# Two unused 32-byte pieces that shift the on-chip placement of a two-block transformer kernel

## The chip, the cores and the metric

The kernel runs on one core of one Trainium2 chip. The metric is the device time of one execution in microseconds (us); the kernel before takes 3251.84 us, the median of three runs (3248.97 to 3255.56). All data are fp32 in DRAM; a working copy lies in the core's on-chip memory, 128 partitions wide, and every tile has one start address that is the same in all partitions.

## The reference

Two transformer blocks follow one another on 256 tokens of width 2048. Cut to what matters:

```python
# block 1
xn = rmsnorm(h, attn_norm)
proj = xn @ w_in                                  # 2048 x 11776
q_a, k_a, v_a, q_r, k_r, v_r, g_r, gate_a, gate_r = split(proj)
y_a = sliding_window_attention(...) @ w_attn_branch
y_r = retention(...) @ w_ret_branch
h = h + (sigmoid(gate_a) * y_a + sigmoid(gate_r) * y_r) @ w_out
hn = rmsnorm(h, ffn_norm)
# PEER: 8 heads x 16 experts per token out of 16384, chosen by top-k of hn @ w_query
u, vv = expert_down[idx], expert_up[idx]          # rows of 2048
h = h + einsum(gates * gelu(einsum(hn, u)), vv)
h = rmsnorm(h, final_norm)
# block 2
z = rms_norm(h, mix_norm) @ w_in_2                # q, k, v, forget gates, recurrent branch
h = h + concat(forgetting_attention(q, k, v, f), rg_lru(conv(rx)) * gelu(rg)) @ w_out_2
h = h + hierarchical_moe(rms_norm(h, ffn_norm_2)) # 32 experts, top 1 group, top 2 in it
h = h + sigmoid(rms_norm(h, ple_norm) @ w_ple_gate) * (p @ w_ple_up)
```

## The kernel before

**One product, three matmuls.** TensorE reads its operands as float32r, a rounded fp32. To keep fp32 accuracy each operand is split into a rounded part `hi` and a rest `lo` (`split`, `split_w`): ScalarE casts the raw weights to `hi` (L251), VectorE subtracts to get `lo` (L252). Each product is then three matmuls into one accumulator: hi by hi, hi by lo, lo by hi. A matmul has a stationary operand, loaded first by LDWEIGHTS (128 by 128 here), and a moving operand that is streamed through (512 columns in most of them).

**Which operand lies where.** Five pools are opened first, in this order: `cst` (constants and small vectors that stay), `big` (seven buffers of 16 KB: activations and their split parts, gathered rows), `sm` (small scratch), `wr` (three raw weight tiles of 8 KB), `ws` (two pairs of `hi` and `lo` of the weights, 4 KB each). Behind them each phase opens pools of its own (`wk...` for work tiles, `wr...` and `ws...` for more weight buffers). A pool begins where the one before it ends, so the size of `cst` and `sm` sets the addresses of all the others.

- `mm_nat` (L272, matmuls L280, L281, L282): the activations in `big` are stationary, the weights in `ws` move, 512 columns. It serves the big input projection (`pj`), the branch products (`pb`), the output products (`pwo`), q and k of block 2 (`pqk`) and the closing gate (`pgt`). For v of block 2 (`pv`) the move is 344 columns wide: a pair of k tiles lies in one `ws` tile, the second 1376 bytes behind the first.
- `mm_tr` (L284, L291 to L293): weights stationary, 256 columns of activations in `big` moving.
- The dense pass over PEER's up table (L805 to L807): coefficients in work tiles (`wk`) are stationary, weights in `ws` or work tiles move, 512 columns. Beside it GpSimd gathers further rows and VectorE adds them.
- The experts of block 2: `gate_up` (L1262, L1279 to L1281) has sorted tokens `xs` in `big` as stationary operand; `down` (L1295, L1304 to L1306) has hidden rows `hhl` in a work tile. Weights in `ws` move, 512 columns, in both.
- PEER's down part gathers one row of 8 KB per token and expert into `big` (L609) and VectorE takes its dot product with `hn` (L619).

**What sets the order.** Each engine works through its own instructions in program order. Weight loads are issued by SyncE, gathers by GpSimd; a load waits until the buffer that it fills has been read.

Of the kernel before, what the change touches and what calls it, by code (L numbers as in the profile page):

```python
# [65 lines left out]
NPU = (7, 5)  # steps of the per-layer embedding's input part before and inside the routing of the experts  # L66
UA = 3  # gathered units added per expert group
NC0 = 1  # chunks of token tile 0's coefficients that stay on chip
# [7 lines left out]
def build(ctx: ExitStack, tc: tile.TileContext, A, out, taps=None, stop=None):  # L76
# [13 lines left out]
    def new_phase(name, raws=0, splits=0, e8=2):  # L90
        """working memory of one phase; raws / splits more buffers for the weight stream"""
        phase.close()
        env["wk"] = phase.enter_context(tc.tile_pool(name="wk" + name, bufs=2, reuse_waits="tile"))
        env["raw"] = [wr0] * 3
        env["split"] = [ws0] * 2
        if raws:
            env["raw"] += [phase.enter_context(tc.tile_pool(name="wr" + name, bufs=raws, reuse_waits="tile"))] * raws
        if splits:
            env["split"] += [phase.enter_context(tc.tile_pool(name="ws" + name, bufs=splits, reuse_waits="tile"))] * splits
        env["ri"] = env["si"] = 0  # L100
        env["e8"] = e8
# [25 lines left out]
    cc = cst.tile([P, NKEEP], F32, name="cc")  # L127
    nc.sync.dma_start(cc[:, 0:128], A["c_const"][:, 0:128])
    vecs = w4([P, P], name="vecs")
    nc.scalar.dma_start(vecs[0:16, :], A["attn_norm"].rearrange("(r c) -> r c", c=P))  # L130
    # input and first weights
# [48 lines left out]
    # gains of the final norm times those of the first norm of block 2  # L180
# [13 lines left out]
    def rsqrt_to(dst, v, n, tag):  # L194
        """dst = v ** -0.5 ([P, n])"""
        if n <= 4:
            G.tensor_tensor(out=dst, in0=v, in1=mhalf[:, 0:n], op=ALU.pow)  # L197
            its = 1
        else:
            d = dst.bitcast(I32)  # L200
            V.tensor_scalar(d, v.bitcast(I32), 1, None, op0=ALU.logical_shift_right)
            V.tensor_scalar(d, d, -1.0, float(0x5F3759DF), op0=ALU.mult, op1=ALU.add)
            its = 3
        tmp = sm.tile([P, n], F32, tag="rs" + tag, name="rs")
        for _ in range(its):
            V.tensor_tensor(out=tmp, in0=dst, in1=dst, op=ALU.mult)
            V.scalar_tensor_tensor(out=tmp, in0=tmp, scalar=-0.5, in1=v, op0=ALU.mult, op1=ALU.mult)
            V.scalar_tensor_tensor(out=dst, in0=tmp, scalar=1.5, in1=dst, op0=ALU.add, op1=ALU.mult)
# [9 lines left out]
    def rstd_from(ss, tag):  # L218
        """ss [P, 2, 4] sums of squares -> rstd [P, 2]"""
        r = cst.tile([P, 2], F32, name="r" + tag)  # L220
        v = sm.tile([P, 2], F32, tag="rstdv", name="rstdv")
        V.tensor_reduce(out=v, in_=ss, axis=AX.X, op=ALU.add)
        V.tensor_scalar(v, v, 1.0 / D, EPS, op0=ALU.mult, op1=ALU.add)  # L223
        rsqrt_to(r, v, 2, "n")
        return r
# [7 lines left out]
    def split(hi, lo, src, scale=None):  # L233
        """hi + lo = src (* scale); hi is rounded to float32r, lo holds the rest"""
        if scale is None:
            return (S.copy(hi, src),
                    V.tensor_tensor(out=lo, in0=src, in1=hi.bitcast(F32), op=ALU.subtract))
        return (S.mul(hi, src, scale),  # L238
                V.scalar_tensor_tensor(out=lo, in0=src, scalar=scale, in1=hi.bitcast(F32),  # L239
                                       op0=ALU.mult, op1=ALU.subtract))  # L240
# [14 lines left out]
    def load_w(src, n=4, w=512):  # L255
        """src [n*128, w] in DRAM -> raw tile [P, n, w]"""
        raw = raw_tile([P, n, w], "raw")
        nc.sync.dma_start(raw, src.rearrange("(k p) n -> p k n", p=P))
        return raw

    def wsplits(W, c0, c1, k0, nk, rot=0, loaded=()):
        """yields (k index, hi [P, w], lo [P, w]) over the k tiles of W[:, c0:c1], the first rot of them last"""
        loaded = list(loaded)
        for g in [*range(rot, nk, 4), *range(0, rot, 4)]:
            n = min(4, nk - g)
            raw = loaded.pop(0) if loaded else load_w(W[(k0 + g) * P:(k0 + g + n) * P, c0:c1], n, c1 - c0)
            for j in range(0, n, 2):
                hi, lo = split_w(raw[:, j:j + 2, :], [P, 2, c1 - c0])
                for i in range(2):
                    yield k0 + g + j + i, hi[:, i, :], lo[:, i, :]  # L270

    def mm_nat(ps, xhi, xlo, W, c0, c1, k0=0, nk=NK, xk=lambda k: k, first=True, last=True, loaded=()):  # L272
        """ps [P, 2, w] (+)= x @ W[:, c0:c1] with tokens on partitions"""
# [10 lines left out]
    def mm_tr(ps, xhi, xlo, W, c0, rot=0):  # L284
        """ps [P, 4, 256] = (x @ W[:, c0:c0+512]) with columns on partitions"""
# [15 lines left out]
    def transposed_split(hi, lo, src, gains, kts=range(NK), n=1):  # L301
        """hi/lo [P, NK, 256] <- transposes of src [P, 2, D] times per-feature gains"""
        for k0 in kts[::n]:
            if k0 % 2 == 0:
                ps = pst("ptr")
            for k in range(k0, k0 + n):
                for t in range(2):
                    o = (k % 2) * 256 + t * P
                    TE.transpose(ps[:, o:o + P], src(t, k), ident)  # L309
            for k in range(k0, k0 + n):  # L310
                o = (k % 2) * 256
                r = split(hi[:, k, :], lo[:, k, :], ps[:, o:o + 256], gains(k))
        return r

    # ================= block 1: projections =================
# [14 lines left out]
    def rope(ps, nh):  # L330
        """ps [P, 2, nh*128] raw projection -> roped, normalised [P, 2, nh, 128] in SBUF"""
# [11 lines left out]
    def heads_T(dst, o, nh, scale=1.0):  # L343
        """dst [P(d), nh, 256] <- o [P(tok), 2, nh, 128]"""
# [18 lines left out]
    for b in range(2):  # L363
        ps = proj(b * 512)
        if b == 0:
            # small constants, once the first products are under way
# [170 lines left out]
    # ================= PEER =================  # L537
# [88 lines left out]
    def key_rows(t):  # L626
        """keys of token tile t with (head, choice) on partitions: [P, 2, token]"""
# [14 lines left out]
    def onehots(dst, kT, tk, n):  # L642
        """dst [P, n, 128] = second keys of n tokens"""
        # 1 where key - iota is 0, else max(1 - (key - iota) ** 2, 0) = 0
# [4 lines left out]
    def coef_chunk(kT, cT, c, oh=None, pool=lambda tk: False):  # L649
        """coefficients of 32 tokens as [second key, first key, token]"""  # L650
# [65 lines left out]
    def onehots_ahead(kT, oh1):  # L716
        """one-hot second keys of most of token tile 1, in buffers that are idle until the dense part"""
# [27 lines left out]
    # rows of 512 columns, the last of the 4 of an expert  # L745
# [26 lines left out]
    def coef_split(ig):  # L772
        """coefficients of the 4 x 128 experts of group ig, experts on partitions: hi, lo [P, 4, 256]"""
# [52 lines left out]
    # final norm of block 1 and first norm of block 2; their scales go to the results  # L826
# [21 lines left out]
    def log1p_of(dst, u, n, tag):  # L848
        """dst = log(1 + u) for 0 <= u <= 1 ([P, n])"""
# [12 lines left out]
    # softplus(-lam) * 8 per channel  # L862
# [23 lines left out]
    for b in range(2):  # L886
        pq = acc("prx").rearrange("p a b -> p (a b)").rearrange("p (m t) -> p m t", m=4)
        mm_tr(pq, zhi, zlo, W2, 3080 + b * 512, 12)
        if b == 0:
# [11 lines left out]
            # r4 of every token on all partitions  # L901
# [57 lines left out]
    v2_ = wv[:, 1, :].rearrange("p (t c) -> p t c", t=2)  # L959
    qkTs = bigt([P, 2, 2, 4, T], name="qkTs")  # L960
    for b in range(3):
        # the columns of v, then the 8 of the forget gates
# [19 lines left out]
    def bias_row(hd):  # L982
        """[tril mask - c_s (keys 0:128) | -c_s (keys 0:128) | tril mask - c_s (keys 128:256)]"""
# [93 lines left out]
    for b in range(4):  # L1077
# [21 lines left out]
        # rows of h for the sort into slots, features in the order of the expert weights  # L1099
# [9 lines left out]
    # the part of the per-layer embedding that depends on its input alone  # L1109
# [27 lines left out]
    # ================= mixture of experts: routing =================  # L1137
# [7 lines left out]
    # 4 groups, 4 of filling, 32 experts  # L1145
# [45 lines left out]
    # in range: group * 128 + rank; beyond: 512 + (rank - 128)  # L1191
# [35 lines left out]
    # group sizes (on every partition); at most one group has more than 128 tokens  # L1227
# [17 lines left out]
    # ================= mixture of experts: experts =================  # L1245
# [4 lines left out]
    def sort(pr, k0, k1):  # L1250
        """rows of h in the slots of two groups, transposed, times the norm gain"""
# [10 lines left out]
    def gate_up(ge_, e, x_, rs_, cm_, between=lambda c: None):  # L1262
        """hidden rows of expert ge_ for 128 slots, times their weights, transposed (hi, lo)"""
# [56 lines left out]
    def run_experts(items, between=lambda i, c: None):  # L1320
        """items: (expert index, position 0..7, x, rstd, weights, PmT) in order, 8 to a group of slots"""
# [28 lines left out]
    def between(i, c):  # L1350
        """the sort, spread over the first experts"""
# [17 lines left out]
    # the first weights of the per-layer embedding  # L1369
# [7 lines left out]
    # tokens beyond the 128 slots of their group  # L1377
# [32 lines left out]
    # ================= per-layer embedding =================  # L1410
# [58 lines left out]
```

## Time and profile before

| what | value |
|---|---|
| median of three runs | 3251.84 us (3248.97 to 3255.56) |
| span of the profiled execution | 3250.5 us |
| TensorE matmul busy | 2585.5 us (80%), 12368 instructions |
| VectorE busy | 2536.2 us (78%) |
| ScalarE busy | 1540.2 us (47%) |
| GpSimd busy | 874.5 us (27%) |
| DMA mean | 276 GB/s, 898.20 MB |

The span is that of one execution under the profiler and lies 1.3 us under the median. The matmuls are pipelined: one of 512 columns is shown with a duration of about 0.39 us while the next starts 0.23 us later, so the time that one costs is read from the distance between starts in the timeline, and not from its duration. The granted clock of TensorE (PEclk) is the share of full speed that it was given in a stretch; 1.00 is the higher of its two levels, 2.4 GHz.

### The profile page before, as it was taken

What the parts mean: (1) busy time and instruction counts of PE and PEld (TensorE: products, weight loads), DVE (VectorE), ACT (ScalarE), POOL (GpSimd) and SP (SyncE); (2) the same over time, 40 slices, a digit from 0 to 9 for tenths busy, and PEclk for the clock granted to TensorE, in tenths of its full rate; (3) what the DMA queues carried; (4) which work ended last, traced back from release to release, by engine and by line L of the source; (5) the groups of instructions that cost most, each with busy time, mean ns of one, the idle gap of its engine ahead of it and who ended that gap; (6) DMA issues with size and microseconds to landing.
All of it is one profiled execution on the core that took longest, in us unless ns stands there. A gap on an engine that the chain in (4) does not pass through costs nothing. (4 is left out here: it accounts for less than half of the span.)

```text
span 3250.5 us, 35193 instructions
## 1 busy us (share of the span) xinstructions
PE 2585.5 (80%) x12368; PEld 2137.8 (66%) x12368; DVE 2536.2 (78%) x3682; ACT 1540.2 (47%) x2212; POOL 874.5 (27%) x575
## 2 busy tenths in 40 slices
PE   8999999999920004400399999999999999999999
PEld 7788788888820003300378888889887787878777
DVE  6656544445899999999988888887575789999974
ACT  5533444444310104442244444457445677777763
POOL 0000000000276686667766666620000000000000
PEclk9999999999965555555699999999999999999999
DMA  6454555555899899989799999964654599999964
GB/s 235 150 178 159 181 181 187 189 207 190 309 376 358 329 421 369 400 336 414 290 310 335 332 335 333 335 240 148 203 181 137 213 336 339 374 341 374 340 230 157
DMA packets 302521, 898.20 MB, mean 276 GB/s; under 512 B 20736, under 2 KB 42240, under 8 KB 268288
## 3 DMA queue, kind: packets, MB, share of 16 engines
q1 hardware_dynamic: 226560, 542.88, 47.3%
q0 software_dynamic: 57760, 335.65, 27.0%
q10 hardware_dynamic: 18016, 17.35, 1.6%
q8 instruction: 98, 1.61, 0.2%
q14 instruction: 87, 0.71, 0.1%
HBM read 887.42 MB, written 8.39 MB: 276 GB/s over the span
## 5 line engine op out<-in xcount | busy, mean ns | idle before, releaser
L252 DVE TENSOR_TENSOR wlo<-raw,whi 128x1024 fp32r<-128x1024 f32 (+1 forms) x538 | 648.3, 1208 | 467.9 <-ACT whi L251 464.1
L251 ACT CAST whi<-raw 128x1024 fp32r<-128x1024 f32 (+1 forms) x538 | 557.0, 1036 | 706.0 <-PE pj L282 267.8
L619 DVE CUSTOM_DVE_ANT_0 row<-row,hn 128x2048 f32<-128x2048 f32 x256 | 578.4, 2282 | 8.9 <-DMA row<-in_peer_expert_down_dram,eidx 7.7
L610 POOL DMA_INDIRECT row<-in_peer_expert_down_dram,eidx x256 | 503.5, 1967 | 270.4 <-DVE dots L619 96.9
L197 POOL TENSOR_TENSOR r<-rstdv,mhalf 128x2 f32<-128x2 f32 x5 | 4.5, 891 | 1535.7 <-DVE rstdv L223 1535.7
L610 POOL DMA_INDIRECT urow<-in_peer_expert_up_dram,eidx x256 | 322.4, 1259 | 196.9 <-DVE h L769 143.3
L252 DVE TENSOR_TENSOR wlo<-rawg,whi 128x1024 fp32r<-128x1024 f32 x256 | 313.2, 1225 | 41.9 <-ACT whi L251 37.4
L251 ACT CAST whi<-rawg 128x1024 fp32r<-128x1024 f32 x256 | 269.3, 1053 | 104.7 <-PE pgu L1281 75.8
L280 PE MATMUL pj<-whi,xhi 128*128 128x512 f32 x736 | 293.0, 398 | 1.3 <-ACT whi L251 1.3
L281 PE MATMUL pj<-wlo,xhi 128*128 128x512 f32 x736 | 292.3, 397 | 0.0
L282 PE MATMUL pj<-whi,xlo 128*128 128x512 f32 x736 | 291.8, 397 | 0.0
L637 PE MATMUL pcf<-cc,pk 128*128 128x128 f32 x2 | 0.9, 462 | 344.1 <-DVE pk L624 344.1
L637 PEld LDWEIGHTS pcf<-cc,pk 128*128 128x128 f32 x2 | 0.4, 183 | 344.9 <-issue 179.2
L1280 PE MATMUL pgu<-wlo,xs 128*128 128x512 f32 x512 | 203.2, 397 | 3.1 <-DVE wlo L252 3.1
L1279 PE MATMUL pgu<-whi,xs 128*128 128x512 f32 x512 | 203.4, 397 | 0.0
L1281 PE MATMUL pgu<-whi,xs 128*128 128x512 f32 x512 | 202.9, 396 | 0.0
L769 DVE SCALAR_TENSOR_TENSOR h<-urow,pk,h 128x512 f32<-128x512 f32 x256 | 191.6, 749 | 4.4
L252 DVE TENSOR_TENSOR wlo<-rawd,whi 128x1024 fp32r<-128x1024 f32 x128 | 154.1, 1224 | 15.7 <-ACT whi L251 11.2
L280 PEld LDWEIGHTS pj<-whi,xhi 128*128 128x128 f32 x736 | 138.2, 188 | 34.2 <-ACT whi L251 1.7
L282 PEld LDWEIGHTS pj<-whi,xlo 128*128 128x128 f32 x736 | 138.1, 188 | 32.7
L281 PEld LDWEIGHTS pj<-wlo,xhi 128*128 128x128 f32 x736 | 138.1, 188 | 32.4
L251 ACT CAST whl<-raw 128x1024 fp32r<-128x1024 f32 x96 | 101.1, 1054 | 114.2 <-PE ua L807 82.4
(547 smaller groups left out, 6287.2 us busy)
## 6 DMA issues: line engine op xcount, KB each, us to landing
raw<-in_w_in_dram SPq DMA_DIRECT2D x124, 1024.0 KB
raw<-in_peer_expert_up_dram SPq DMA_DIRECT2D x96, 1024.0 KB
rawg<-in_w_expert_gate_dram SPq DMA_DIRECT2D x128, 512.0 KB
rawg<-in_w_expert_up_dram SPq DMA_DIRECT2D x128, 512.0 KB
rawd<-in_w_expert_down_dram SPq DMA_DIRECT2D x64, 1024.0 KB
raw<-in_w_out_dram SPq DMA_DIRECT2D x32, 1024.0 KB
raw<-in_w_ret_branch_dram SPq DMA_DIRECT2D x16, 1024.0 KB
raw<-in_w_peer_query_dram SPq DMA_DIRECT2D x16, 1024.0 KB
```

What stands on the lines that cost most here:

```text
L197: G.tensor_tensor(out=dst, in0=v, in1=mhalf[:, 0:n], op=ALU.pow)
L251: S.copy(hi, raw)
L252: env["last"] = V.tensor_tensor(out=lo, in0=raw, in1=hi.bitcast(F32), op=ALU.subtract)
L280: TE.matmul(ps[:, t, :], h_, hi, start=st, stop=False)
L281: TE.matmul(ps[:, t, :], h_, lo, start=False, stop=False)
L282: env["mm"] = TE.matmul(ps[:, t, :], l_, hi, start=False, stop=en)
L610: G.indirect_dma_start(out=dst, out_offset=None, in_=src, in_offset=bass.IndirectOffsetOnAxis(ap=idx, axis=0))
L619: V.tensor_tensor_reduce(out=row[:, i, :], in0=row[:, i, :], in1=hn[:, t, :], scale=1.0, scalar=0.0, op0=ALU.mult, op1=ALU.add, accum_out= ...
L769: V.scalar_tensor_tensor(out=h[:, t, 1536:2048], in0=row[:, k, :], scalar=coef[:, t, c0 + k:c0 + k + 1], in1=h[:, t, 1536:2048], op0=ALU.m ...
L1279: TE.matmul(o_, xh, hi[:, :, i, :], start=k == 0, stop=False)
L1280: TE.matmul(o_, xh, lo[:, :, i, :], start=False, stop=False)
L1281: TE.matmul(o_, xl, hi[:, :, i, :], start=False, stop=k == NK - 1)
```

## The change

Two tiles of 8 fp32 numbers are added that nothing reads or writes, one in `cst` behind `cc` and one in `sm`. A tile in `sm` is there twice (`bufs=2`), so `cst` grows by 32 bytes and `sm` by 64. Every other line of the diff drops a comment or a docstring; behind L126 all lines move down by two.

```diff
     cc = cst.tile([P, NKEEP], F32, name="cc")
+    cst.tile([P, 8], F32, name="pad")
+    sm.tile([P, 8], F32, tag="pad", name="pad")
     nc.sync.dma_start(cc[:, 0:128], A["c_const"][:, 0:128])
```

The instructions of all five engines, their order, their shapes and their waits are the same as before. What differs is the start of the tiles. In the built programs, in bytes per partition:

| tiles | before | after | before mod 256 | after mod 256 |
|---|---|---|---|---|
| `cc` (in `cst`, ahead of the piece) | 16512 | 16512 | 128 | 128 |
| `big`, seven buffers in steps of 16384 | 23008 | 23040 | 224 | 0 |
| `wr`, three in steps of 8192 | 140960 | 141056 | 160 | 0 |
| `ws`, `hi` and `lo`, in steps of 4096 | 165536 | 165632 | 160 | 0 |
| work tiles of the phases, first one | 181920 | 182016 | 160 | 0 |
| `hhl` (experts, down) | 192160 | 192256 | 160 | 0 |
| `chi` (PEER up) | 207520 | 207616 | 160 | 0 |
| second k tile of a 344-wide weight pair (first `ws` tile) | 166912 | 167008 | 0 | 96 |

By 512 bytes the remainders after are 0 for `big` and 256 for `wr`, `ws` and the work tiles; before, 480 and 160.

## Rows read from the trace of the kernel before

**Rows 1.** The page: span, and the granted TensorE clock in 40 slices.

```profile
span 3250.5 us, 35193 instructions
...
PEclk9999999999965555555699999999999999999999
```

**Rows 2.** Busy time by stretch: PE, PEld, DVE, ACT, POOL; then PEclk, DMA share, GB/s.

```profile
81.00:812.60 731.60, 731.58 (x3269) 588.48 (x3269) 391.17 (x477) 316.38 (x388) 6.22 (x9) 1.00 0.53 180
...
975.00:1560.00 585.00, 69.30 (x261) 55.94 (x261) 573.69 (x957) 146.64 (x380) 402.61 (x208) 0.51 0.96 377
1645.00:2150.00 505.00, 505.00 (x2229) 418.31 (x2228) 437.95 (x613) 239.10 (x368) 309.69 (x246) 1.00 0.97 336
2195.00:2520.00 325.00, 317.64 (x1813) 276.44 (x1812) 214.00 (x371) 178.71 (x257) 0.00 (x0) 1.00 0.50 168
2600.00:3090.00 490.00, 485.02 (x2127) 389.75 (x2126) 444.70 (x427) 371.93 (x404) 0.00 (x0) 1.00 0.95 351
```

**Rows 3.** Timeline of PE, block 1, 430 to 450: first and last of 87.

```profile
429.76 0.39 PE L281 MATMUL pj<-wlo,xhi 128*128 128x512 f32 x1
...
449.83 0.39 PE L280 MATMUL pb<-whi,rhi 128*128 128x512 f32 x1
```

**Rows 4.** Timeline of PE, PEER's up part, 1800 to 1820: first and last of 90.

```profile
1799.82 0.39 PE L805 MATMUL ua<-whi,chi 128*128 128x512 f32 x1
...
1819.99 0.39 PE L807 MATMUL ua<-whi,clo 128*128 128x512 f32 x1
```

**Rows 5.** Timeline of PE, experts, 2700 to 2714: six steps of down, 47 of gate_up.

```profile
2700.49 0.39 PE L1306 MATMUL oa<-whi,hhl 128*128 128x512 f32 x1
...
2701.85 0.39 PE L1306 MATMUL oa<-whi,hhl 128*128 128x512 f32 x1
2702.07 0.40 PE L1279 MATMUL pgu<-whi,xs 128*128 128x512 f32 x1
...
2713.04 0.39 PE L1281 MATMUL pgu<-whi,xs 128*128 128x512 f32 x1
```

**Rows 6.** Timeline of PE, 344 columns: starts of three k tiles, six matmuls each.

```profile
2268.17 0.32 PE L280 MATMUL pv<-whi,zhi 128*128 128x344 f32 x1
...
2269.11 0.32 PE L280 MATMUL pv<-whi,zhi 128*128 128x344 f32 x1
...
2270.07 0.32 PE L280 MATMUL pv<-whi,zhi 128*128 128x344 f32 x1
```

**Rows 7.** Groups of PE by line and shape: busy, mean ns, idle before them.

```profile
L280 PE MATMUL pj<-whi,xhi 128*128 128x512 f32 x736 | 293.0, 398 | 1.3 <-ACT whi L251 1.3
...
L1279 PE MATMUL pgu<-whi,xs 128*128 128x512 f32 x512 | 203.4, 397 | 0.0
...
L1304 PE MATMUL oa<-whi,hhl 128*128 128x512 f32 x256 | 101.5, 396 | 0.0
...
L805 PE MATMUL ua<-whi,chi 128*128 128x512 f32 x256 | 100.1, 391 | 0.5 <-ACT chi L236 0.5
...
L291 PE MATMUL pq<-hhi,whi 128*128 128x256 f32 x256 | 72.5, 283 | 0.0
```

**Rows 8.** Groups of DVE by line and shape: one operation at shifts of 4 bytes.

```profile
L917 DVE SCALAR_TENSOR_TENSOR rnx<-rnx,vt 128x255 f32<-128x255 f32 x8 | 3.5, 477 | 0.0
L917 DVE SCALAR_TENSOR_TENSOR rnx<-rnx,vt 128x253 f32<-128x253 f32 x8 | 3.5, 476 | 0.0
```

**Rows 9.** DMA queue of weights, 406 to 487 and 2330 to 2400: packets, MB, share.

```profile
q1 hardware_dynamic: 7458, 14.78, 53.5%
...
q1 hardware_dynamic: 5458, 10.82, 45.8%
```

**Rows 10.** DMA queue of gathers, 1143 to 1215 and 1480 to 1540: packets, MB, share.

```profile
q0 software_dynamic: 4155, 30.26, 101.3%
...
q0 software_dynamic: 3393, 24.67, 100.7%
```

**Rows 11.** DMA queue of weights in the experts, 2762 to 2844: packets, MB, share.

```profile
q1 hardware_dynamic: 8230, 30.49, 99.0%
```

## The prediction

> **What bounds the kernel now.** I read the page's slices first, then busy time by stretch, and then went down to the distance between the starts of matmuls, because nothing but addresses changes and no view of waits can show that.
>
> The stretches [rows 2] fall into three kinds. In block 1 (81 to 812.6) the matmuls are busy for 731.58 of 731.60 us at the full granted clock, with DMA at 0.53 and VectorE at 391 us: TensorE is the only bound. The first half of block 2 (2195 to 2520) is alike, 317.64 of 325 us, DMA 0.50. In PEER's up part (1645 to 2150) and in the experts (2600 to 3090) TensorE is full as well (505 of 505, 485 of 490), but DMA stands at 0.97 and 0.95, so a faster TensorE meets a second limit at once. PEER's gathers (975 to 1560) are VectorE's: 573.69 of 585 us, TensorE 69 us at a granted clock of 0.51.
>
> A full TensorE need not be TensorE at its peak, so I took what one matmul costs from start to start. In block 1, 86 steps take 449.83 - 429.76 = 20.07 us, 233.4 ns each [rows 3]. In PEER's up part 89 steps take 1819.99 - 1799.82 = 20.17 us, 226.6 ns each [rows 4]. These are the same instruction (128 by 128 stationary, 512 columns, float32r) at the same full clock: 560 cycles of 2.4 GHz against 544. The experts show both figures within 14 us [rows 5]: down takes (2701.85 - 2700.49)/6 = 226.7 ns, gate_up right behind it (2713.04 - 2702.07)/47 = 233.4 ns. Weights come through the same buffers in both, DMA is busy in both. What differs is where the stationary operand lies. In the groups at 233.4 ns (L280 to L282, L1279 to L1281) it is in `big`, 224 past a multiple of 256, while the moving one is at 160. In those at 226.7 (L805 to L807, L1304 to L1306) both are at 160.
>
> The 344-column matmuls give a second handle [rows 6]. Their stationary operand is in `big` throughout, the moving one lies at 160 for one k tile and at 0 for the next. Six matmuls take 2269.11 - 2268.17 = 0.94 us for one and 2270.07 - 2269.11 = 0.96 us for the other, 156.7 and 160.0 ns. (The rounding of one start is 0.01 us; the pattern 0.94, 0.96 repeats over the following tiles.) In cycles that is 376 against 384, or 32 over the 344 columns against 40; with 512 columns it is 32 over against 48. So addresses matter, the better state is 32 cycles over the columns, and it was reached in two ways: with both operands at one remainder, or, as I read the order of the pairs, with the moving operand on a multiple of 256. After the change both hold in all of the groups at 233.4.
>
> **The change part by part.** Instructions added: none; removed: none; waits: the same. Each term is a number of matmuls by 233.4 - 226.7 = 6.7 ns.
>
> - Block 1. `pj` has 736 matmuls on each of the three lines [rows 7]; `pb` has 192 and block 1's `pwo` 128 in groups of the same form. (736 + 192 + 128) x 3 = 3168, by 6.7 ns: 21.2 us. All of it lies on the path: PE idles 1.3 us for ScalarE before the 736 of L280 [rows 7], and the two splitting engines have room, 316 and 391 us of 731 [rows 2]. What is late next is nothing: DMA would go from 0.53 to 0.55.
> - Block 2 outside the experts. Block 2's `pwo`, `pqk` and `pgt` with 128 each, x 3 = 1152: 7.7 us. Same reasoning, DMA 0.50 in the first part.
> - Experts, gate_up. 512 x 3 = 1536 [rows 7]: 10.3 us if TensorE alone decides. DMA's mean of 0.95 over 490 us [rows 2] would rise to 0.97 and fits on the mean, but in 82 us in the middle the weights' queue already takes 99.0% of the 16 engines [rows 11]; there a faster TensorE waits for weights. Bounds 0 and 10.3; I take half, 5 us, since the mean leaves room for all and the middle for almost nothing.
> - Experts, down: 256 x 3 = 768, at 226.7 in [rows 5]. 0 taken; should they start at 233.4 behind every gate_up, at most half of 768 x 6.7, 2.6 us.
> - PEER's up part: 2304 matmuls (256 on each of three lines for `ua` from one kind of buffer [rows 7], as many from the other, and half as many each for `ub`). At 226.6 now: 0.
> - `mm_tr`: 512 x 3 = 1536 of 256 columns (`pq` [rows 7] and two groups of 128). The moving operand goes from 224 to 0. No pair of rows tells whether these can be faster; by the same excess per column the end is 1536 x 3.35 = 5.1 us, the other end 0. I take 0, since [rows 7] show nothing unequal there.
> - 344 columns: 288 matmuls. The first k tile of a pair moves to 0 and the second to 96, so the better and the worse half change places: 0, give or take 0.5 us.
> - VectorE and ScalarE: operands move by 32 or 96 bytes. One operation ran at shifts of 4 to 12 bytes in 477 and 476 ns [rows 8], so I price all of them at 0. This is the term that the gathers' stretch rests on (573.69 us of VectorE): 1% there would be 5.7 us either way.
> - DMA: destinations move from 224 or 160 to 0. On the reading side two layouts can be compared. Rows of block 1's table have a pitch that is a multiple of 256 in DRAM, those of block 2's a pitch of 80 x 256 + 32. A packet took 81 us x 16 x 0.535 / 7458 = 93.0 ns in the one and 70 x 16 x 0.458 / 5458 = 94.0 in the other [rows 9], about 1%. I price the writing side at 0.
>
> [...]
>
> Sum: 21.2 + 7.7 + 5 = 33.9 us off the profiled span of 3250.5 [rows 1], 3216.6. The median is 1.3 above that span, so 3218 us.
>
> **The rivals.**
>
> *No change (about 3251).* The two spacings are due to something else that goes with the groups: the source buffers, the accumulator, the way the stationary operand is strided. For it: I infer from a few placements, none of which is the new one (0 for both, and by 512 still 0 against 256). Against it: [rows 6], where only the moving address alternates. To this case belongs a gain on DMA alone. [...] VectorE bounds most of the gathers, and DMA only where its queue takes all of the time: 72 and 60 us at 101.3 and 100.7% [rows 10]. [...]
>
> [...]
>
> *Slower (3272).* The spacing of 226.7 belongs to the offset 160 itself, or to some pairing that the new grid breaks: operands that all start on a multiple of 256 collide, and these groups fall to 233.4 and the others stay. Place: L805 and L1304. Price: 2304 x 6.7 = 15.4 and 768 x 6.7 = 5.1, together 20.5 us, and all on the path, since TensorE is full there [rows 2]: 3251.8 + 20.5 = 3272. It decides when L805 has 233 ns between starts. For it: those stationary and moving operands leave exactly the layout that gives 226.7 now. Against it: they keep equal remainders, and the moving operand at 0 was the better one in [rows 6].
>
> *Much faster (3170).* The 32 cycles that remain are an address cost too. At 512 cycles, 213.3 ns, all groups gain; half of it, 220 ns, gives block 1 and 2 (4320 matmuls) 13.4 x 4320 = 58 us, and the up part and the experts what DMA leaves, 3% of 505 and 5% of 490, up to 40. A sum near 80, 3170. For it: every starting address is off the grid today but one. Against it: that one ([rows 6], moving at 0) still had 32 over.
>
> **How the numbers follow.** The forecast 0.50, no change 0.24, slower 0.16, much faster 0.07, and 0.03 for gains and losses that cancel to a few us. One such measurement can tell about 0.2%, 6.5 us, from no change. Faster: 0.50 + 0.07 and a third of the rest, 0.58. Same: 0.26. Slower: 0.16. The likeliest case alone runs from 3205 (with all of gate_up, down and `mm_tr`: 33.9 + 5.3 + 2.6 + 5.1 = 46.9) to 3235 (half of the sum). The range goes from 3200 to 3273, so that it holds no change and the slower case as well and leaves out the much faster one and some tails.
>
> **What would show it.** In the profile after: starts in block 1's 512-column matmuls 226.7 ns apart, block 1's stretch 21 us shorter, the experts' between 0 and 10; L805 still at 226.6; the 344-column pairs with 0.94 and 0.96 in exchanged places; mean durations of L252, L619 and L251 unchanged; the mean packet of the weights' queue unchanged. I am wrong if block 1 keeps 233.4 (then addresses weren't it), if L805 rises (slower), if any spacing falls under 226, or if VectorE's L619 moves.

## The result, and the profile after

The changed kernel takes 3213.97 us (median of 4 runs, 3209.80 to 3219.45) where the kernel before, on the same chip, takes 3251.30: a ratio of 0.9884, 95% interval 0.9870 to 0.9898. On a second occasion it was 3214.33 and 0.9888 (0.9873 to 0.9903). The forecast was 3218 us, so 33 to 34 us of gain, and some 37 came.

The page, with the same two rows as [rows 1]: the span is 32.8 us shorter, the clock the same.

```profile
span 3217.7 us, 35193 instructions
...
PEclk9999999999965555555699999999999999999999
```

The timeline of PE in block 1, first and last of 90 (line numbers are two higher than before):

```profile
429.63 0.39 PE L283 MATMUL pj<-wlo,xhi 128*128 128x512 f32 x1
...
449.81 0.39 PE L282 MATMUL pb<-whi,rhi 128*128 128x512 f32 x1
```

(449.81 - 429.63)/89 = 226.7 ns, where [rows 3] gave 233.4. In PEER's up part nothing has moved, 20.17/89 = 226.6 as in [rows 4]:

```profile
1799.73 0.39 PE L808 MATMUL ua<-whl,chi 128*128 128x512 f32 x1
...
1819.90 0.39 PE L807 MATMUL ua<-whl,chi 128*128 128x512 f32 x1
```

In the experts gate_up, the second half of [rows 5], goes from 233.4 to (2688.54 - 2679.70)/39 = 226.7 ns:

```profile
2679.70 0.39 PE L1283 MATMUL pgu<-whi,xs 128*128 128x512 f32 x1
...
2688.54 0.39 PE L1283 MATMUL pgu<-whi,xs 128*128 128x512 f32 x1
```

The 344-column pairs of [rows 6] hardly alternate any more. By the starts in the trace the two k tiles of a pair took 0.960 and 0.940 us before and mostly take 0.950 and 0.943 after. The first two:

```profile
2248.02 0.32 PE L282 MATMUL pv<-whi,zhi 128*128 128x344 f32 x1
...
2248.96 0.32 PE L282 MATMUL pv<-whi,zhi 128*128 128x344 f32 x1
...
2249.90 0.32 PE L282 MATMUL pv<-whi,zhi 128*128 128x344 f32 x1
```

In the groups of [rows 7] the durations shrink by 5 to 6 ns where a group gained, while that of `pq` in `mm_tr` grows by 5:

```profile
L282 PE MATMUL pj<-whi,xhi 128*128 128x512 f32 x736 | 289.4, 393 | 1.3 <-ACT whi L253 1.3
...
L1281 PE MATMUL pgu<-whi,xs 128*128 128x512 f32 x512 | 200.0, 391 | 0.0
...
L293 PE MATMUL pq<-hhi,whi 128*128 128x256 f32 x256 | 73.7, 288 | 2.0 <-ACT whi L253 2.0
```

For a balance I took the mean distance between successive starts in each group, leaving out steps over 300 ns (200 in `mm_tr`), which are waits:

| group | matmuls | before, ns | after, ns | difference x matmuls, us | forecast, us |
|---|---|---|---|---|---|
| block 1: `pj`, `pb`, `pwo` | 3168 | 233.3 | 226.7 to 227.2 | -20.0 | -21.2 |
| block 2: `pqk`, `pwo`, `pgt` | 1152 | 233.3 | 226.8 to 227.8 | -6.8 | -7.7 |
| gate_up | 1536 | 233.3 | 227.2 | -9.4 | -5 |
| down | 768 | 229.6 | 227.7 | -1.5 | 0 |
| PEER up | 2304 | 226.7 | 226.7 | 0 | 0 |
| `mm_tr` | 1536 | 117.8 | 120.0 | +3.4 | 0 |

That is 34.3 us. One stage adds to it: from the last `pq` matmul to the first of the up part, in which VectorE and the gathers decide, 717.0 us went by before and 713.0 after (714.2 on the second occasion).

The two together come to 38.3, which is more than the 32.8 by which these two profiles differ: the table prices every matmul as if all of it were on the path. Cut into stages, the same two profiles give, in us: block 1 up to the first `pq` -18.6, `pq` +4.7, the gathers' stage -4.0, the up part +1.6, `prx` with `prg` -2.0, the rest of block 2 up to the experts -1.9, the experts -11.0, the closing gate to the end -2.5, and +1.1 in the pieces between. The profiled execution after was the slowest of its four (3219.45); the repeat, which ran 7 us shorter, gives -17.7, +1.3, -2.8, -0.2, -1.4, -3.3, -9.3, -5.0 and -1.3.

### The profile page after: what moved, and what is told of

The parts are those of the page before. It is cut to its first block, busy times and chain, and to the rows that moved or that the text cites. A ratio compares the mean times of both kernels' runs of the same rounds, so it can differ in the third digit from the quotient of the medians.

```text
span 3217.7 us, 35193 instructions
## 1 busy us (share of the span) xinstructions
PE 2555.4 (79%) x12368; PEld 2141.8 (67%) x12368; DVE 2535.2 (79%) x3682; ACT 1542.9 (48%) x2212; POOL 879.8 (27%) x575
## 5 line engine op out<-in xcount | busy, mean ns | idle before, releaser
L621 DVE CUSTOM_DVE_ANT_0 row<-row,hn 128x2048 f32<-128x2048 f32 x256 | 579.7, 2291 | 6.1 <-DMA row<-in_peer_expert_down_dram,eidx 5.7
L254 DVE TENSOR_TENSOR wlo<-rawg,whi 128x1024 fp32r<-128x1024 f32 x256 | 313.1, 1225 | 35.1 <-ACT whi L253 10.3
L1281 PE MATMUL pgu<-whi,xs 128*128 128x512 f32 x512 | 200.0, 391 | 0.0
L1283 PE MATMUL pgu<-whi,xs 128*128 128x512 f32 x512 | 199.2, 389 | 0.0
```

Of the source, the lines that this page charges most:

```text
L254: env["last"] = V.tensor_tensor(out=lo, in0=raw, in1=hi.bitcast(F32), op=ALU.subtract)
L621: V.tensor_tensor_reduce(out=row[:, i, :], in0=row[:, i, :], in1=hn[:, t, :], scale=1.0, scalar=0.0, op0=ALU.mult, op1=ALU.add, accum_out= ...
L1281: TE.matmul(o_, xh, hi[:, :, i, :], start=k == 0, stop=False)
L1283: TE.matmul(o_, xl, hi[:, :, i, :], start=False, stop=k == NK - 1)
```

## The experiments

Three theories stood at the start. 1: the distance between the starts of the stationary and the moving operand decides, counted by 256 bytes. 2: the moving operand has to start on a multiple of 256. 3: the stationary operand at 224 is the fault by itself. Each of the first three kernels keeps the condition of one theory and breaks the others.

**Only the piece in `cst`.** `big` comes to 0, `ws` and the work tiles to 192: the distance stays.

```diff
+    cst.tile([P, 8], F32, name="pad")
```

> Only the piece in cst: big starts at a multiple of 256, ws and the work tiles at 192 past one. Theory 1 (the distance between stationary and moving operand decides, by 256 bytes): the distance in the groups with the stationary operand in big stays 64 as before, so 512-column matmuls of L280 stay at 233 ns and the time at 3251 us. Theory 2 (the moving operand has to start on a multiple of 256): 192 is none, 233 ns, 3251 us; should a multiple of 64 be enough, 226.7 ns and 3214. Theory 3 (the stationary operand in big at 224 was the fault by itself): 226.7 ns, 3214 us. PEER's up part keeps equal remainders: 226.6 ns by theory 1.

3248.98 us against 3254.33, ratio 0.9987 (0.9977 to 0.9997). Block 1's 87 starts are (449.88 - 429.82)/86 = 233.3 ns apart:

```profile
429.82 0.39 PE L283 MATMUL pj<-whi,xlo 128*128 128x512 f32 x1
...
449.88 0.39 PE L282 MATMUL pb<-wlo,rhi 128*128 128x512 f32 x1
```

Theory 3 falls: the stationary operand is at 0 and nothing is gained in the matmuls. The few microseconds that were gained, 4 by the ratio with an interval from 1 to 7, come up again below.

**Only the piece in `sm`.** `big` stays at 224, the rest comes to 224: distance 0, far off the grid of 256.

```diff
+    sm.tile([P, 8], F32, tag="pad", name="pad")
```

> Only the piece in sm: big stays at 224 past a multiple of 256, ws and the work tiles come to 224 as well, off every grid of 64. Theory 1 (distance): distance 0, so L280 at 226.7 ns and about 3214 us, the whole gain. Theory 2 (moving operand on a multiple of 256): no gain, 233 ns, 3251 us; the up part may even get worse. Theory 3 (stationary operand at 224 at fault): no gain, 3251 us, and the up part, whose stationary operand comes to 224, goes to 233 ns, 15 us more, 3266.

3221.27 us, ratio 0.9903 (0.9886 to 0.9920); 90 starts, (449.99 - 429.81)/89 = 226.7 ns:

```profile
429.81 0.39 PE L281 MATMUL pj<-whi,xhi 128*128 128x512 f32 x1
...
449.99 0.39 PE L283 MATMUL pb<-whi,rlo 128*128 128x512 f32 x1
```

Theory 2 and theory 3 fall, theory 1 stands. Whether the whole gain is here can't be told from the time: the kernel before took 3254.33 beside it, so that the change's ratio of 0.9884 would have given about 3217, and the two intervals overlap.

**Moving operand on the grid.** `big` at 224, the rest where the change puts it.

```diff
+    sm.tile([P, 24], F32, tag="pad", name="pad", bufs=1)
```

> An unused piece of 96 bytes in sm alone: big stays at 224, ws and the work tiles come to a multiple of 256, as they are after the change. Theory 1 (distance, here 224): no forecast of its own for a distance of 224; in the 344-column pairs of before this distance gave 156.7 against 160.0 ns, so L280 would be near 226.7 and the time near 3214 to 3220. Theory 2 (moving operand on a multiple of 256): 226.7 ns, 3214 us. Theory 3 (stationary at 224 at fault): 233 ns, 3251 us.

3249.98 us, ratio 0.9991 (0.9981 to 1.0000); 87 starts, (449.85 - 429.78)/86 = 233.4 ns:

```profile
429.78 0.39 PE L282 MATMUL pj<-wlo,xhi 128*128 128x512 f32 x1
...
449.85 0.39 PE L281 MATMUL pb<-whi,rhi 128*128 128x512 f32 x1
```

Theory 2 falls here too. Theory 1 had no figure for a distance of 224, and my guess for it from 344 columns, near 226.7, missed. This also disposes of my reading of [rows 6], by which a moving operand at 0 was the better one as such.

**A map of start addresses.** Matmuls alone, all else left out.

> Leaves out the whole computation: matmuls alone, 30 back to back for each pair of start addresses of stationary and moving operand in steps of 32 bytes, over 512 bytes with 512 columns, over 256 bytes with 344 and 256 columns. Theory 1 (distance): the distance between starts of 512-column matmuls is 226.7 ns on the diagonal of equal remainders and larger off it, repeating each 256 bytes or less along both axes, and depends on the difference alone. Theory 2 (moving on the grid): 226.7 in the columns of moving starts at 0 and 256 whatever the stationary start. Theory 3: 226.7 or 233 by the stationary start alone. A fourth outcome is that all pairs give one figure; then the two figures need something of the kernel that this one lacks.

Mean distance between the last 15 starts of each cell, in ns, read from the trace; the 512-byte map repeats by 256 along both axes to 1 ns but for four cells, so rows of its first corner stand for it (stationary start down, moving start across, 512 columns):

```
          0     32     64     96    128    160    192    224
  0   226.6  233.4  228.9  233.4  232.4  234.3  233.4  233.4
 32   233.4  226.6  233.5  228.9  233.4  232.4  234.3  233.4
 64   233.4  233.4  226.6  233.4  228.9  233.4  233.4  234.3
160   233.4  232.4  234.3  233.3  233.4  226.7  233.2  228.9
224   233.5  228.7  233.5  232.4  234.3  233.3  233.4  226.6
```

Equal remainders give 226.7 in every cell, a moving operand 64 further on 228.9, all else 232 to 234. Of the four cells that don't repeat, two lie at a distance of 64 (stationary at 0 or 256, moving at 320) and give 233.3. The kernel before was the cell 224, 160: 233.3. With 256 columns the diagonal is among the worst instead: 120.0 ns, and 113.3 to 120.1 off it; the cell of `mm_tr` before (160, 224) gives 117.8, the kernel's own figure. With 344 columns the cells lie between 153 and 160, the diagonal at 157.6 to 157.8 but for one cell (64, 64) at 153.4.

**The up part set apart.** A change in the opposite sense, in a stage that the edit left alone.

```diff
     new_phase("p")
+    env["wk"].tile([P, 8], F32, tag="pad", name="pad", bufs=1)
```

> The changed kernel with one more unused piece of 32 bytes, in the work pool of PEER's phase only: the coefficients chi and clo and the split weights whl of the up part come to 32 past a multiple of 256, the ws tiles stay on one. Nothing else moves. Theory 1 (distance by 256 bytes, as in the map): the matmuls of the up part that move whi and wlo of ws (1152 of 2304, distance 224) go from 226.7 to 233.4 ns, those that move whl (distance 0) stay; 1152 x 6.7 = 7.7 us, about 3222 against 3214. Rival (the up part is bound by transfers or by VectorE's additions as soon as the matmuls change, and the spacing there is no price): the spacings as above, but no more than 2 us on the time. Rival (the grid of 256 decides): all 2304 off 226.7, 15 us.

3221.09 us beside 3214.33 of the changed kernel beside it, 6.8 more. The matmuls on `whi` and `wlo` step by (1805.05 - 1799.68)/23 = 233.5 ns. Those on `whl` begin with steps of 230 and settle at (1810.52 - 1807.80)/12 = 226.7:

```profile
1799.68 0.40 PE L808 MATMUL ua<-whi,chi 128*128 128x512 f32 x1
...
1805.05 0.40 PE L810 MATMUL ua<-whi,clo 128*128 128x512 f32 x1
1805.29 0.39 PE L808 MATMUL ub<-whl,chi 128*128 128x512 f32 x1
...
1807.80 0.39 PE L810 MATMUL ub<-whl,clo 128*128 128x512 f32 x1
...
1810.52 0.39 PE L810 MATMUL ub<-whl,clo 128*128 128x512 f32 x1
```

The intervals of the two whole times overlap, so the stage has to decide. From its first to its last `ua` matmul it took 528.4 us here, and 519.1 to 521.4 in the seven other kernels and repeats. So distance is a price on the path there too, and neither transfers nor VectorE hide it.

**A distance of 64.**

```diff
+    cst.tile([P, 8], F32, name="pad")
+    sm.tile([P, 32], F32, tag="pad", name="pad", bufs=1)
```

> big on a multiple of 256, ws and the work tiles 64 past one: for the 512-column matmuls of L280 and gate_up the moving operand lies 64 behind the stationary one, for mm_tr (weights stationary) 64 ahead of it. If the map carries over to the kernel: 512 columns at 228.8 ns (most cells of that distance) or 233.4 (the cell of exactly these remainders by 512), 256 columns at 113.3 ns instead of 120.0. Against the changed kernel: 5856 x 2.2 = 12.9 us or 5856 x 6.7 = 39 us lost, 1536 x 6.7 = 10 us gained, so 3217 or 3243 us. If the map does not carry over: 3214 (mm_tr and L280 as after) or 3251.

3224.75 us, ratio 0.9922 (0.9908 to 0.9935). The spacings came as in most cells of that distance, 89 starts at (449.96 - 429.82)/88 = 228.9 ns in block 1 and, with 256 columns, 73 at (2247.89 - 2239.73)/72 = 113.3. The cell of exactly these remainders by 512 (0 and 320) has 233.3 in the map, so a single cell doesn't carry over to the kernel. And the time is 10 us over the changed kernel and not 3:

```profile
429.82 0.39 PE L284 MATMUL pj<-whi,xlo 128*128 128x512 f32 x1
...
449.96 0.39 PE L282 MATMUL pb<-whi,rhi 128*128 128x512 f32 x1
...
2239.73 0.28 PE L293 MATMUL prg<-zhi,whi 128*128 128x256 f32 x1
...
2247.89 0.28 PE L293 MATMUL prg<-zhi,whi 128*128 128x256 f32 x1
```

Set beside the repeat of the changed kernel, block 1 up to the first `pq` lost 5.8 us (777.7 against 771.9), near what its spacing says, but `pq` itself gained only 1.9 (110.7 against 112.6) and `prx` with `prg` 0.7 (106.1 against 106.8), of 8.4 that their spacing is worth. In `mm_tr` part of what a shorter matmul saves turns into waiting. PE's wait in `pq` for VectorE's `wlo` is 8.8 us in the repeat and 11.9 here:

```profile
PE pq L295 <- DVE wlo L254: 8.8, 15, 2.3
...
PE pq L295 <- DVE wlo L254: 11.9, 14, 2.6
```

**The changed kernel again.**

> The changed kernel unaltered, beside the others on the same chip: 3214 us, 0.988 to 0.989 of before. If its gain were chance of one chip, the ratio would go towards 1.

3214.33 us, ratio 0.9888: the gain is the same to 0.1%.

**Fine steps.** Matmuls alone.

> Leaves out the whole computation: matmuls alone. First, 512 columns with the distance in steps of 4 bytes from -68 to 68: theory 1 in its sharp form has 226.7 ns at distance 0 alone and 233 already at 4 bytes; in its coarse form a plateau as wide as some piece of memory (up to 32 bytes either way, since the first map went in steps of 32). Should some distance fall under 226.7, there is more to gain. Second, stationary starts alternate between 0 and 96 and moving starts with them or against them. If a matmul's own stationary operand has to be at distance 0, alternating together gives 226.7 and against each other 233; if the stationary operand that is loaded meanwhile for the next matmul has to be at distance 0, it is the other way round. Third, widths 128 to 512 at distances 0, 96 and 192: if distance 0 costs 32 cycles over the columns at every width, it is the worst of the three at 256 and the best at 512.

No distance of 35 is under 226.6, so the much faster case that I had as a rival is not there. There is no plateau either, and 0 is not the only distance at 226.7: -4, 28 and 60 have it too. With 512 columns and the stationary operand at 128, moving operand minus stationary above, mean of the last 15 steps in ns below:

```
 -16    -12     -8     -4      0      4      8     12     16     20     24     28     32
233.3  240.0  233.4  226.7  226.7  236.6  233.3  228.9  231.9  236.0  233.3  226.7  233.3
```

The program goes through all distances twice. Two distances came out differently in the two passes, -68 with 226.7 and 230.2 and -60 with 233.3 and 240.0, so the two addresses alone don't fix the step.

Alternating both starts between 0 and 96 together gave 234 ns, alternating them against each other 230. By a matmul's own distance the first would be 226.7; so that is not what is paid for. By the distance to the weights loaded meanwhile the second would be 226.7, and it is only half way there. With 128 and with 192 columns the step is 111.5 to 111.9 ns at all three distances tried, so something other than the columns sets it there. Above that the best distance changes with the width. Of the three (0, 96 and 192), 0 is the best at 384 columns (173.3 against 176.7 and 176.8), no better or worse at 320 (146.7 each) and the worst at 448 (206.7 against 205.3 and 202.3).

**One odd matmul in 16.** To see whose distance it is.

> Leaves out the whole computation: 512-column matmuls alone, both operands at remainder 0, but one in 16 has its stationary or its moving operand 96, 32 or 116 bytes further on. Theory A (a matmul pays for the distance between its own two operands): with the stationary operand odd in number 8, the distance from start 8 to start 9 rises from 226.7 to 234 ns, and the same one with the moving operand odd. Theory B (it pays for the distance to the weights that are loaded for the next matmul while it streams): with the stationary operand odd in number 8, the distance from start 7 to start 8 rises, by some 7 ns at 96, and with the moving operand odd that from 8 to 9. Theory C (a state of the stream that needs several equal matmuls): no single distance rises, several do, before or behind.

Distances from start to start in ns; number 8 is the odd one, the same in each repeat but for 1 ns:

```
step from             6    7    8    9   10   11   12   13   14   15
stationary +96      227  229  230  236  229  232  231  227  226  227
stationary +32      227  235  228  233  231  226  227  227  226  227
stationary +116     227  231  231  230  236  229  232  231  227  226
moving +96          227  226  236  230  236  228  233  231  226  227
moving +32          227  226  236  233  233  236  224  231  236  228
```

An odd stationary operand is felt one matmul early, in number 7, which streams while the weights of number 8 are loaded (in the kernel before, the load for the matmul that starts at 440.26 us begins at 440.03 and takes 0.19, beside the matmul that starts at 440.03); an odd moving operand is felt in its own. That is the place that theory B names, though not its size: at 96 the step from 7 rises by 2 ns and not by 7. And one odd matmul also disturbs the next three to nine, which is theory C. It costs from 20 ns in all for a stationary operand at 32 (235 + 228 + 233 + 231 - 4 x 226.7) to some 50 for a moving one at 32, with about 30 for either at 96. So an effect in the stream outlives the address that caused it. That this is why alternating patterns don't come out as the mean of two cells is likely, but not shown.

**The remaining microseconds.** The kernels already run bear on these, by their profiles. The stage from the last `pq` to the first `ua` takes 716.6 to 718.3 us in the three kernels with `big` off the grid of 256 and 713.0 to 714.2 in the five profiles with it on. Inside it, the starts of the 16th and the 240th of PEER's dot products (L619 before) lie 641.5 to 641.9 us apart in the three and 638.8 to 639.4 in the five. VectorE itself is not faster in them. The dot product takes 2281 to 2283 ns in seven of the eight profiles and 2291 in that of the changed kernel; what shrinks is its idle time ahead of a dot product, nearly all of it a wait for rows, from 8.9 to 9.5 us in the three to 6.1 to 7.4 in the five. Before, after, and the repeat of after:

```profile
L619 DVE CUSTOM_DVE_ANT_0 row<-row,hn 128x2048 f32<-128x2048 f32 x256 | 578.4, 2282 | 8.9 <-DMA row<-in_peer_expert_down_dram,eidx 7.7
```

```profile
L621 DVE CUSTOM_DVE_ANT_0 row<-row,hn 128x2048 f32<-128x2048 f32 x256 | 579.7, 2291 | 6.1 <-DMA row<-in_peer_expert_down_dram,eidx 5.7
```

```profile
L621 DVE CUSTOM_DVE_ANT_0 row<-row,hn 128x2048 f32<-128x2048 f32 x256 | 577.7, 2282 | 6.7 <-DMA row<-in_peer_expert_down_dram,eidx 6.2
```

Of the 8192-byte packets of the gathers those that took up to 310 ns are 45% before, 49% with the piece in `sm` alone and 50% in the third kernel, where `big` is at 224; with `big` at a multiple of 256 they are 90% (piece in `cst` alone) and 91% (both). Of the rest most of the undisturbed ones took 312 to 314 before, most of the others up to 321. In the same 70 us (1130 to 1200), the queue of gathers of before, of the third kernel, of the one with `cst` alone, of the one with `sm` alone, and after:

```profile
q0 software_dynamic: 4003, 29.19, 100.8%
```

```profile
q0 software_dynamic: 4009, 29.18, 101.2%
```

```profile
q0 software_dynamic: 4087, 29.77, 100.8%
```

```profile
q0 software_dynamic: 4041, 29.44, 101.3%
```

```profile
q0 software_dynamic: 4116, 29.93, 101.2%
```

In the first three the stage begins at about the same time, in the last two some 15 us earlier; with `big` on the grid it is 2% more packets in either set. So some 3.5 us of the stage (the pairs of kernels differ by 2.4 to 5.3) go with the start of `big`. The whole times don't separate them: the piece in `cst` alone has 3248.98 us and the third kernel, with `big` off the grid, 3249.98. With `big` at 224 about half of the packets pay some 4 of 309 ns, 1.3%. Why only half of them pay stays open.

## Why the prediction was right, point by point

- *What bounds the kernel; the two spacings are a matter of addresses; equal remainders give 226.7.* Right, and shown by one kernel for each alternative. Of the two ways by which I thought the better state was reached, only the distance holds. The alternation of 0.02 us in [rows 6] was real, but I read a grid into it. The map has 156.6 for that 344-column cell (224, 0), no better than its neighbours, and 157.7 for the other (224, 160), where the kernel had 160.0; why the second differs is open.
- *Block 1 21.2, block 2 7.7.* 20.0 and 6.8 by the starts, and 18.6 or 17.7 in block 1's stretch up to the first `pq`. Mis-sized: in the changed kernel too the first matmuls after a wait step by 231 to 236 ns before they settle at 226.7.
- *Gate_up 5 of 10.3.* Too low: 9.4, and the experts' stage (first `pgu` to last `oa`) went from 580.0 to 569.0 us, 570.7 on the repeat. With the piece in `sm` alone, which leaves the weights' buffers off the grid, it is 569.6, so this gain is the matmuls' and not that of the transfers. What failed was the reading that a faster TensorE would find the weights' queue full, because it stood at 99.0%. In the 82 us around the same place after the change it carries more packets at the same share, 8377 where [rows 11] have 8230 (why is not shown):

```profile
q1 hardware_dynamic: 8377, 31.08, 99.3%
```

- *Down 0.* 1.5 us, within its bound. The cause is open: that `down` follows a gate_up at 226.7 is not it alone, since in the third kernel gate_up still steps by 233.3 and `down` by 227.9.
- *`mm_tr` 0, with an end at 5.1 us of gain.* Wrong in sign: 117.8 to 120.0 ns, 3.4 us if all of it were on the path. The bound assumed that one excess per column holds at every width; the map shows that the distance that is best at 512 columns is among the worst at 256. How much of it reached the end can't be told: the `pq` stretch went from 111.2 to 115.9 and, on the repeat, 112.6 us, while `prx` with `prg` went from 108.2 to 106.2 and 106.8.
- *344 columns: halves exchanged.* They became nearly equal, 158.3 and 157.2 ns a matmul, worth 0.2 us over all 288.
- *VectorE and ScalarE 0.* Right. L252 stays at 1223 ns; L619 goes from 2282 to 2291 in the first profile after, but is at 2282 in the repeat, so that is not the change. L251 goes from 1049 to 1054 and 1052.
- *DMA, writing side 0.* Mis-sized: the gathers' stage became 3 to 4 us shorter; a gain on DMA I had put with the rival of no change and not in the sum. The reading-side pair that I leaned on says nothing on where a packet is written. For the weights' 2048-byte packets 0 holds: the median is 84 ns in every profile.
- *Rivals.* The slower one fell with the up part's 226.6, the much faster one with the maps. The cycle that the forecast counts in, 1/2.4 ns, is what a column costs here at a granted clock of 1.00: (226.6 - 156.7)/(512 - 344) = 0.416 ns by [rows 4] and [rows 6]. In the maps the steps at distance 0 with 256, 320, 384 and 512 columns, 120.0, 146.7, 173.3 and 226.7 ns, are 0.417 ns a column and 13.3 on top, 32 such cycles; 448 columns, at 206.7, lie 6.7 above that line. What the 13.3 ns are is not shown.

In the sum the errors cancel: gate_up and down +5.9, DMA +3.5, `mm_tr` and the two blocks -5.5. The mechanism was right; that the total came within 4 us is in part luck.

## What to carry to other kernels

Measure a full engine from start to start: here a matmul that streamed 512 columns in 233 ns in one place and in 227 in another, at a granted clock of 1.00 in both, was an address effect, and two such places in one trace were enough to forecast it. Here the thing to set is the distance between the operand that streams and the weights loaded beside it, for the width that dominates, and another width may want the opposite (distance 0 gave 226.7 ns with 512 columns, where none was under 226.6, and 120.0 with 256, where others gave down to 113.3). A piece of padding moves every tile behind it, here by 32 or 96 bytes, so try each piece alone before telling what it did: of these two, the one in `sm` alone gives the matmuls their gain, at a small price in `mm_tr`, and the one in `cst` gives the gathers theirs.

## What the hardware showed that was not expected

- The time of a matmul depends on the remainder by 256 of two start addresses against each other, from 226.7 to 240.0 ns with 512 columns in steps of 4 bytes, and from 113.3 to 120.1 with 256 columns in steps of 32. Why 256 and why this pattern stays open.
- A single odd address is paid for over several matmuls, 20 to 50 ns in all.
- Gathered packets of 8192 bytes that go to a multiple of 256 bytes take up to 310 ns in 90% of cases; 224 past one, only about half do, and most of the others take 312 to 321.
